# Moving the steps of the weights' sums between the stages of a decoder layer

## The chip, the cores and the metric

The kernel runs on one core of one Trainium2 chip. The metric is the device time of one execution in microseconds (us), the median of the runs shown. All stages run on the same five engines: PE (TensorE, the matmuls), ACT (ScalarE), DVE (VectorE), POOL (GpSimd) and SP (SyncE, which here only issues DMAs). ACT and POOL issue DMAs too, each in the order of its own instructions.

## The reference, cut to what matters

One layer is computed for a prompt of 1024 tokens and for 8 x 8 decode tokens, 1088 columns in all, with a model width of 1024. All is fp32.

```
hn = rmsnorm(x);  u = hn @ w_in                      # q,k,v, gates of both branches
o_a = forgetting attention(q_a, k_a, v_a, logf)      # 8 heads of 64
o_b = gated linear attention(q_b, k_b, v_b, alpha)   # 4 heads, 128 x 256
merged = sigmoid(gate_a) * (o_a @ w_proj_a) + sigmoid(gate_b) * (o_b @ w_proj_b)
x = x + rmsnorm(merged @ w_out)
u = rmsnorm(x) @ w_up;  conv of width 3 over the tokens
y = x + rmsnorm((gelu(g) * a) @ w_down)
```

The product with `w_up` (1024 x 5632) is done for the first 768 tokens with sums of blocks: of each pair of column blocks of `w_up`, four half blocks x11, x12, x21, x22 are added up in four combinations, and these sums take part in seven products instead of eight. The sums depend on the weights alone. They can be made at any time before the stage that multiplies by `w_up`.

## The kernel before, in words

The stages follow each other: the first norm, the forget gates, the attention of the prompt (called FoX here, about 95 to 455 us of the profile), the attention of the decode tokens (to about 640), the linear attention (GLA, four heads, to about 1045), the merge of the branches (to about 1163), the output projection with its norms (to about 1293), the up-projection (to about 1740) and the down-projection. Each fp32 product is made as three products of fp32r halves: `hi` (ACT) and `lo` (DVE or POOL) split an operand, and `three` multiplies.

**The sums of the weights.** They are made by DMAs alone, from HBM to HBM, into the tiles `d_ws[i]`, four of 256 KB for each i from 2 to 21. `ws_step(a, b)` does one step, n = 2, 3, 4 and so on, one n for each call. ACT issues four plain copies of blocks of `w_up` into `d_ws[n]` (L195), placed behind the instruction `a` of ACT. POOL issues up to four adding DMAs (L200), placed behind the instruction `b` of POOL: two from `w_up` into `d_ws[n-1]`, one into `d_ws[n-2]` from a tile of the same i and one into `d_ws[n-3]`, likewise. Each of these waits until the DMA of the step before that wrote its operand has landed. Calls beyond n = 24 issue nothing, and from n = 22 only POOL issues.

**FoX.** Four pairs of heads j; within a pair 16 iterations n, each one tile of 128 queries of a head. In an iteration the scores of the next tile are made (POOL masks the diagonal block, L722, DVE adds and finds the maximum, ACT takes the exponential, L745), then the tile before it is transposed (`pth`, `ptl`) and multiplied with the values. Between these, `slot()` puts in a written-out share of projection matmuls (`mm`), whose weights SP loads (`wraw`) and which hide the softmax; the order of PE's matmuls is fixed by hand. `ws_step(*pace)` is called at n = 1, 4, 7, 10 and 13, with `pace` the last exponential and the last mask. SP also copies `d_sfb`, HBM to HBM, eight times here.

**GLA.** One more call for each head, behind the exponential and the subtraction that make the decayed queries. These are steps 22 to 25.

**The merge.** For each of 8 blocks m of output channels, SP loads the weights (`wraw`, 512 KB), the gate (`sg`, 544 KB) and the first branch's product (`m1`, shown as `m`, 544 KB). ACT takes the sigmoid of `sg` (L1391), PE multiplies in three groups of 384, 384 and 320 columns, and for each group `ev` has DVE multiply by the gate, POOL add `m1`, ACT split off the high half and DVE the low half. `sg` and `m1` have two buffers each, `whi` and `wlo` two, and the PSUM pool of the products three. The operands `bh`, `bl` of the merge are eight blocks k loaded from `d_ob` just ahead of it.

The engines' orders come from a scheduler that walks the program with estimated costs; `tc.issue_after(x)` only says that what is issued in it stands behind x on its engine. DMAs of SP and ACT share eight semaphores in turn, and one that takes a semaphore waits for the DMA that used it before.

Of the kernel before, what the change touches and what calls it, by code (L numbers as in the profile page):

```python
# [10 lines left out]
AF = mybir.ActivationFunctionType  # L11
ALU = mybir.AluOpType
# [7 lines left out]
T = 1024  # L20
# [72 lines left out]
def hybrid_step(ctx, tc, I, O):  # L93
    nc = tc.nc
    pe, act, dve, pool, sp = nc.tensor, nc.scalar, nc.vector, nc.gpsimd, nc.sync
# [10 lines left out]
    def f(ap):  # L106
        return ap.bitcast(F32)
# [19 lines left out]
    def tt(eng, out, a, b, op):  # L127
        eng.tensor_tensor(out=out, in0=a, in1=b, op=op)  # L128
# [7 lines left out]
    def lo(out, src, h, eng=dve):  # L136
        tt(eng, out, src, f(h), ALU.subtract)
# [43 lines left out]
    def ws_step(a, b):  # L181


        n = ws_next[0]
        ws_next[0] += 1

        def x(i):
            wc = [w["w_up"][:, q * P:(q + 1) * P].rearrange("(k p) m -> p k m", p=P) for q in (i, NF + i)]
            return [c[:, k:k + 4] for c in wc for k in (0, 4)]

        with tc.issue_after(a.ins):
            if n in d_ws:
                x11, x12, x21, _ = x(n)
                for d, y in zip(d_ws[n], (x21, x11, x11, x12)):
                    act.dma_start(out=d, in_=y)  # L195
        with tc.issue_after(b.ins):
            for i, d, y in ((n - 3, 3, None), (n - 2, 1, None), (n - 1, 0, 3), (n - 1, 2, 2)):
                if i in d_ws:
                    src = x(i)[y] if y else d_ws[i][{3: 1, 1: 0}[d]]
                    pool.dma_start(out=d_ws[i][d], in_=src, max_dma_last_dim=4 * P * 4, accum_op=ALU.add)  # L200

    ws_next, pace = [2], [None, None]
# [197 lines left out]
    def mgroup(g, wh, wl, evac, M=P, rh=None, rl=None, K=KD):  # L400
        rh, rl = rh or hn_h, rl or hn_l
        o, n = GS[g]
        ps = new(ps_mm, [P, 384], "mm")
        ins = three(ps[:M, :n], [(wh[:, k, :M], wl[:, k, :M], rh[g][:, k, :], rl[g][:, k, :]) for k in range(K)])
        evac(ps, o, n)
        return ins

    def mtile(*args, **kw):
        for g in range(3):
            mgroup(g, *args, **kw)  # L410
# [27 lines left out]
    def w_col(col):  # L438
        return lambda: load_split(wpool, w["w_in"][:, col:col + P], KD, P)
# [27 lines left out]
    def enqueue_fill(n=1):  # L467
        for _ in range(min(n, len(fillers))):
            col, dst = fillers.pop()
            enqueue(w_col(col), lambda dst=dst: spill(dst))  # L470
# [4 lines left out]
    def barrier():  # L475
        bg.append(("B", None))
# [30 lines left out]
    def drain():  # L507
        units(1 << 30)
# [124 lines left out]
    def fox_q(j, t):  # L633

        qd = t["qd"] = [new(foxk, [P, T], f"qd{h}", F32R) for h in range(2)]

        def ev_q(ps, o, n):
            m = min(n, T - o)
            for h in range(2):
                a, b = 64 * h, 64 * (1 - h)  # L640
                act.activation(qd[h][a:a + 64, o:o + m], ps[a:a + 64, :m], AF.Copy, scale=0.125)
                stt(qd[h][b:b + 64, o:o + m], ps[a:a + 64, :m], 0.125, f(qd[h][a:a + 64, o:o + m]),
                    ALU.mult, ALU.subtract)
                if m < n:
                    act.activation(qb[a:a + 64, :, j, 16 * h:16 * h + NS],
                                   ps[a:a + 64, m:n].rearrange("p (b t) -> p b t", t=NS), AF.Copy, scale=0.125)
        return ev_q
# [134 lines left out]
    def fox_jobs(j, t):  # L782
        enqueue(w_col(C_KA + j * P), lambda: fox_kv(j, t, "k"))
        later(lambda: fox_k_out(j, t))
        enqueue(w_col(C_VA + j * P), lambda: fox_kv(j, t, "v"))
        later(lambda: fox_v_out(j, t))
# [10 lines left out]
    for j in range(4):  # L797
        if j < 3:
            fox_jobs(j + 1, tj[j + 1])
        enqueue_fill(FILL_FOX[j])  # L800
        if j < 3:
            barrier()
            enqueue(w_col(C_QA + (j + 1) * P), lambda j=j: fox_q(j + 1, tj[j + 1]))
        slot = spread(SLOTS_FOX + ([8, 4, 4] if j == 3 else []))
        for n in range(16):
            h, qt = 2 * j + n // 8, n % 8
            scores, turn, values = heads[h]
            if n == 7:
                heads[h + 1] = fox_head(j, 1, tj[j])
            if n < 15:  # L810
                heads[2 * j + (n + 1) // 8][0]((qt + 1) % 8)
                if n % 3 == 1:
                    ws_step(*pace)
                slot()
                if qt == 0 and n:
                    heads[h - 1][2](3)
                if qt % 2 == 0 and qt >= 2:
                    values(qt // 2 - 1)
                slot()
                turn(qt)  # L820
                slot()
                if n == 0 and j == 0:
                    suffix_sums()
                if j in (1, 2) and n % 4 == 2:
                    repeat_sums(4 * (j - 1) + n // 4)
            elif j < 3:
                drain()
                bg.pop(0)
                units(4)
                turn(7)  # L830
                fox_split(j + 1, tj[j + 1])
                units(4)
                values(3)
                act.dma_start(out=d_oa[j], in_=tj[j]["oT"])
                units(4)
                heads[h + 1] = fox_head(j + 1, 0, tj[j + 1])
                heads[h + 1][0](0)
            else:
                slot()
                turn(7)  # L840
                slot()
                values(3)
                slot()
                act.dma_start(out=d_oa[j], in_=tj[j]["oT"])
# [203 lines left out]
    with mkpool(name="gla", bufs=1, side="right") as gp:  # L1048
# [9 lines left out]
        for h in range(HB):  # L1058
            q, k, bc = (gh[h][x] for x in ("q", "k", "bc"))
# [123 lines left out]
            drain()  # L1183
            kth, ktl = (new(gp, [P, TT], "wv", F32R, bufs=5)[:, :T].rearrange("p (c t) -> p c t", t=P) for _ in range(2))
            qe = new(gp, [P, TT], "vT")
            pace[0] = act.activation(qe, bc, AF.Exp, scale=1.0 / 16)
            eb = new(gp, [P, 16], "eb")
            dve.tensor_copy(eb[:, :8].unsqueeze(2), qe[:, :T].rearrange("p (c t) -> p c t", t=P)[:, :, P - 1:])
            dve.tensor_copy(eb[:, 8:].unsqueeze(2), qe[:, T:].rearrange("p (c t) -> p c t", t=NS)[:, :, NS - 1:])
# [2 lines left out]
            qh, ql = (new(gp, [P, TT], "wv", F32R, bufs=5)[:, :T] for _ in range(2))  # L1192
# [9 lines left out]
            for i0 in (0, 4, 8):  # L1202
                ps = new(ps_a, [P, 4, P], "tp")
                n, m = (P, 4) if i0 < 8 else (TS, 1)
# [5 lines left out]
                    lo(ktl[:, i0:i0 + m, :], ps, kth[:, i0:i0 + m, :])  # L1210
                else:
                    stack(ps[:n, 0, :], k3, lambda r: (32 * r, None, 64, 32 - 32 * r))
            pace[1] = pool.tensor_tensor(out=ql, in0=qe[:, :T], in1=f(qh), op=ALU.subtract)
            ws_step(*pace)
            sil = []

            def gate(v):
# [152 lines left out]
    with mkpool(name="mg", bufs=2, side="right") as mg, mkpool(name="obp", bufs=1, side="right") as obp:  # L1370
        bh, bl = zip(*([new(obp, [P, KD, n], f"b{x}{g}", F32R) for x in "hl"] for g, (_, n) in enumerate(GS)))
        sg0 = new(mg, [P, TT], "sg")
        for k in range(KD):
            if k in (0, 1):
                raw = new(wpool, [P, UP], "spl")[:, :TT]
            else:
                raw = new(mg, [P, TT], "sg" if k == 4 else "m1")
            sp.dma_start(out=raw, in_=d_ob[k])
            for g, (o, n) in enumerate(GS):
                hi(bh[g][:, k, :], raw[:, o:o + n])  # L1380
                lo(bl[g][:, k, :], raw[:, o:o + n], bh[g][:, k, :], pool if g == 2 else dve)
        drain()
        mh, ml = new_act()
        m2 = last2[0]
        for m in range(KD):
            wh, wl = load_split(wpool, w["w_proj_b"][:, m * P:(m + 1) * P], KD, P)
            sg = new(mg, [P, TT], "sg") if m else sg0
            sp.dma_start(out=sg, in_=d_gb[m])
            m1 = new(mg, [P, TT], "m1")
            sp.dma_start(out=m1, in_=d_m1[m])  # L1390
            act.activation(sg, sg, AF.Sigmoid)  # L1391

            def ev(ps, o, n):
                g = o // 384
                c = slice(o, o + n)
                tt(dve, sg[:, c], ps[:, :n], sg[:, c], ALU.mult)
                tt(pool, sg[:, c], sg[:, c], m1[:, c], ALU.add)
                hi(mh[g][:, m, :], sg[:, c])
                if g < 2:
                    lo(ml[g][:, m, :], sg[:, c], mh[g][:, m, :])  # L1400
                else:

                    lo(ml[g][:, m, :TS], sg[:, T:], mh[g][:, m, 2 * P:])
                    lo(ml[g][:, m, TS:], sg[:, o:T], mh[g][:, m, :2 * P])

            if m == KD - 1:
                load_wo(0, 0, first_wo)
            mtile(wh, wl, ev, rh=bh, rl=bl)
            if m == 2:
                conv_operands()  # L1410

# [374 lines left out]
    with mkpool(name="dr", bufs=1, side="left") as dr, mkpool(name="ds", bufs=1, side="left") as ds, \  # L1786
# [183 lines left out]
        for hf in range(2 * NS_):  # L1970
# [44 lines left out]
            if (name, h) in (("h12", 1), ("s4", 0)):  # L2015
                c = int(name == "s4")
# [38 lines left out]
```

## Time and profile before

| What | Value |
|---|---|
| Runs | 2013.24, 2014.16, 2023.12 us; median 2014.16 |
| Profiled execution | 2014.25 us, its span 2012.5 us |
| Mean granted clock of TensorE | 0.997 |
| Busy: PE, DVE, ACT, POOL | 97%, 65%, 45%, 20% |
| DMA | 335.24 MB, mean 167 GB/s |

The span runs from the first to the last instruction on the core. The busy share of an engine is averaged over all stages. A row of the timeline has its start and its length in us, then engine, line, operation, tiles and shapes, and in brackets the idle time of its engine before it with what ended that.

### The profile page before, as it was taken

The page shows a single profiled execution, that of the slowest core. Times are in us where ns is not written, and L with a number is a line of the kernel's source. Part 1 is how long each engine was busy: PE and PEld are TensorE (multiplying, and loading weights), DVE is VectorE, ACT ScalarE, POOL GpSimd, SP SyncE. Part 2 cuts the span into 40 slices and gives each one's busy share as a digit, 9 for nine tenths or more (in the row PEclk, how much of TensorE's full clock was granted, in tenths as well). Part 3 has the DMA queues.
Part 4 walks back from the last instruction along what each step waited for, and adds up shares of the span by engine and source line. Part 5 has one row for each costly group of instructions (what it writes and reads, how often), then busy time and mean ns, then how long its engine had stood idle before and what let it go on. Part 6 is the DMA issues. An engine that isn't in the chain of part 4 may idle for free.

```text
span 2012.5 us, 35502 instructions
## 1 busy us (share of the span) xinstructions
PE 1952.2 (97%) x13681; PEld 1788.5 (89%) x13681; DVE 1303.1 (65%) x2635; ACT 914.3 (45%) x1762; POOL 411.8 (20%) x582
## 2 busy tenths in 40 slices
PE   6999999999999999999999999999999999999998
PEld 5899989997888988898989977899999999977886
DVE  6566666663333876867564357876777777848685
ACT  5344444453333565564633243454444444545552
POOL 3022323232110111111012211232233233210000
PEclk9999999999999999999999999999999999999999
DMA  4387979797774252323387352134335555667574
GB/s 140 95 195 179 235 177 194 175 230 256 286 267 145 62 130 55 117 60 106 136 273 234 109 172 101 55 120 159 124 127 171 183 170 193 213 191 242 181 250 154
DMA packets 302430, 335.24 MB, mean 167 GB/s; under 512 B 23327, under 2 KB 234575, under 8 KB 298165
## 3 DMA queue, kind: packets, MB, share of 16 engines
q1 hardware_dynamic: 216501, 217.37, 35.0%
q0 software_dynamic: 39488, 79.15, 15.5%
q10 hardware_dynamic: 46272, 36.44, 5.7%
q8 instruction: 108, 1.77, 0.4%
q14 instruction: 61, 0.50, 0.1%
HBM read 265.78 MB, written 113.30 MB: 188 GB/s over the span
## 4 chain that ended last, share of the span: by engine, by line
PE 82%; DVE 6%; DMA 6%; ACT 4%; issue 1%; ACTq 1%; POOL 0%; SPq 0%; DVEq 0%; POOLq 0%
PE mm L122 40%; PE dn L122 15%; PE u L122 9%; PE tp L125 5%; PE o L122 5%; PE S L122 4%; PE y L122 3%; PE sm L122 1%; DMA d_ob<-oo 1%; ACTq L195 1%; DMA smk<-in_consts 1%; DVE wlo L128 1%; DMA m<-d_ob 1%; DVE act L128 0%; ACT whi L134 0%
## 5 line engine op out<-in xcount | busy, mean ns | idle before, releaser
L122 PE MATMUL mm<-act,whi 128*128 128x384 f32 (+2 forms) x3568 | 893.4, 331 | 5.2 <-DVE act L128 3.9
L122 PEld LDWEIGHTS mm<-act,whi 128*128 128x128 f32 (+1 forms) x3568 | 616.8, 188 | 16.6 <-DVE act L128 5.4
L122 PE MATMUL mm<-act,wlo 128*128 128x384 f32 (+2 forms) x1784 | 582.7, 327 | 0.0
L122 PEld LDWEIGHTS mm<-act,wlo 128*128 128x128 f32 (+1 forms) x1784 | 335.8, 188 | 1.7 <-issue 1.2
L128 DVE TENSOR_TENSOR wlo<-wraw,whi 128x1024 fp32r<-128x1024 f32 (+1 forms) x111 | 131.9, 1189 | 57.4 <-ACT whi L134 54.1
L134 ACT ACTIVATE whi<-wraw 128x1024 fp32r<-128x1024 f32 (+1 forms) x113 | 116.0, 1027 | 92.9 <-PE mm L122 85.1
L131 DVE SCALAR_TENSOR_TENSOR cv<-u,cw,cv 128x1104 f32<-128x1104 f32 x84 | 112.7, 1362 | 13.6 <-ACT cv L1555 13.6
L122 PE MATMUL dn<-dh,hhi 128*128 128x512 f32 x264 | 104.9, 399 | 2.4 <-ACT hhi L134 2.4
L122 PE MATMUL dn<-dh,hlo 128*128 128x512 f32 x264 | 104.9, 397 | 0.3 <-DVE hlo L128 0.3
L122 PE MATMUL dn<-dl,hhi 128*128 128x512 f32 x264 | 105.0, 398 | 0.0
L122 PE MATMUL y<-wo,act 128*128 128x512 f32 x416 | 99.8, 397 | 1.6 <-DVE wo L128 1.1
L122 PEld LDWEIGHTS y<-wo,act 128*128 128x128 f32 x416 | 77.1, 188 | 21.5 <-DVE wo L128 2.2
L134 ACT ACTIVATE sh<-sr 128x512 fp32r<-128x512 f32 x80 | 50.6, 633 | 85.7 <-PE u L122 39.9
L722 POOL TENSOR_SCALAR_AFFINE_SELECT bd<-cb 128x128 f32<-128x128 f32 x64 | 36.8, 584 | 182.7 <-DVE mx L739 166.3
L745 ACT ACTIVATE s<-s,ng 128x128 f32<-128x128 f32 (+3 forms) x64 | 49.6, 776 | 49.0 <-DVE ng L743 46.5
L420 ACT ACTIVATE spl<-mm 128x384 f32<-128x384 f32 (+1 forms) x72 | 33.5, 467 | 78.7 <-PE mm L122 77.7
L735 DVE CUSTOM_DVE_ANT_0 s<-S,cb 128x512 f32<-128x512 f32 (+2 forms) x80 | 40.7, 526 | 40.4 <-PE S L122 32.7
L134 ACT ACTIVATE pth<-tp 128x512 fp32r<-128x512 f32 (+2 forms) x96 | 43.5, 488 | 50.8 <-issue 19.7
L122 PE MATMUL mm<-bh,whi 128*128 128x384 f32 (+1 forms) x192 | 63.1, 328 | 2.8 <-ACT bh L134 1.9
L1555 ACT ACTIVATE cv<-u,cw 128x1104 f32<-128x1104 f32 x42 | 54.9, 1310 | 22.0 <-DVE u L131 11.1
L122 PE MATMUL mm<-bl,whi 128*128 128x384 f32 (+1 forms) x192 | 62.9, 327 | 0.1
L122 PE MATMUL mm<-bh,wlo 128*128 128x384 f32 (+1 forms) x192 | 62.6, 327 | 0.3 <-DVE wlo L128 0.3
(470 smaller groups left out, 4210.4 us busy)
## 6 DMA issues: line engine op xcount, KB each, us to landing
wraw<-in_w_in SPq DMA_DIRECT2D x52, 512.0 KB
wraw<-in_w_up SPq DMA_DIRECT2D x44, 512.0 KB
d_ws<-in_w_up ACTq DMA_DIRECT2D x80, 256.0 KB
sr<-d_ws SPq DMA_DIRECT2D x80, 256.0 KB
draw<-in_w_down SPq DMA_DIRECT2D x77, 256.0 KB
d_h<-cv POOLq DMA_DIRECT2D x44, 256.0 KB, 5.0
d_s<-spl POOLq DMA_DIRECT2D x44, 256.0 KB, 5.2
d_ws<-in_w_up POOLq DMA_DIRECT2D x40, 256.0 KB, 8.2
```

Source lines behind the costliest of these rows:

```text
L122: return record(pe.matmul(out, **kw))
L125: return record(pe.transpose(*args))
L128: eng.tensor_tensor(out=out, in0=a, in1=b, op=op)
L131: return dve.scalar_tensor_tensor(out=out, in0=a, scalar=s, in1=b, op0=op0, op1=op1)
L134: act.activation(out, src, AF.Copy)
L195: act.dma_start(out=d, in_=y)
L420: act.activation(t[:, o:o + n], ps[:, :n], AF.Copy)
L722: pace[1] = pool.affine_select(out=bd, in_=cb[:, qc], pattern=[[-1, P]], compare_op=ALU.is_ge, fill=NEG, base=0, channel_multiplier=1)
L735: dve.tensor_tensor_reduce(out=s[:, k0:k0 + m], in0=ps[:, :m], in1=cb[:, k0:k0 + m], scale=1.0, scalar=-3.0e38, op0=ALU.add, op1=ALU.max, ...
L745: pace[0] = act.activation(s[:, :nk], s[:, :nk], AF.Exp, bias=ng, accum_out=sm)
L1555: act.activation(c, u[:, 2:], AF.Identity, scale=cw[:, 2, m:m + 1], bias=cw[:, 3, m:m + 1])
```

## The change

Three of the calls of `ws_step` are placed otherwise; what a step does is the same. In FoX it is called at n = 1, 5, 9 and 13, 16 times instead of 20. In GLA it is no longer called. In the merge it is called after each of the first seven blocks m, with the block's sigmoid on ACT and the block's last addition on POOL as the instructions to stand behind. That makes 23 calls, steps 2 to 24, where there were 24. FoX then issues the copies of i = 2 to 17, the merge those of i = 18 to 21 (m = 0 to 3) and the adding DMAs of steps 18 to 24: four for each of m = 0 to 4, two for m = 5, one for m = 6. The number of DMAs in all stays 80 of each kind.

```diff
--- before.py
+++ after.py
@@ -809,7 +809,7 @@
                 heads[h + 1] = fox_head(j, 1, tj[j])
             if n < 15:
                 heads[2 * j + (n + 1) // 8][0]((qt + 1) % 8)
-                if n % 3 == 1:
+                if n % 4 == 1:
                     ws_step(*pace)
                 slot()
                 if qt == 0 and n:
@@ -1183,7 +1183,7 @@
             drain()
             kth, ktl = (new(gp, [P, TT], "wv", F32R, bufs=5)[:, :T].rearrange("p (c t) -> p c t", t=P) for _ in range(2))
             qe = new(gp, [P, TT], "vT")
-            pace[0] = act.activation(qe, bc, AF.Exp, scale=1.0 / 16)
+            act.activation(qe, bc, AF.Exp, scale=1.0 / 16)
             eb = new(gp, [P, 16], "eb")
             dve.tensor_copy(eb[:, :8].unsqueeze(2), qe[:, :T].rearrange("p (c t) -> p c t", t=P)[:, :, P - 1:])
             dve.tensor_copy(eb[:, 8:].unsqueeze(2), qe[:, T:].rearrange("p (c t) -> p c t", t=NS)[:, :, NS - 1:])
@@ -1210,8 +1210,7 @@
                     lo(ktl[:, i0:i0 + m, :], ps, kth[:, i0:i0 + m, :])
                 else:
                     stack(ps[:n, 0, :], k3, lambda r: (32 * r, None, 64, 32 - 32 * r))
-            pace[1] = pool.tensor_tensor(out=ql, in0=qe[:, :T], in1=f(qh), op=ALU.subtract)
-            ws_step(*pace)
+            lo(ql, qe[:, :T], qh, pool)
             sil = []
 
             def gate(v):
@@ -1388,13 +1387,13 @@
             sp.dma_start(out=sg, in_=d_gb[m])
             m1 = new(mg, [P, TT], "m1")
             sp.dma_start(out=m1, in_=d_m1[m])
-            act.activation(sg, sg, AF.Sigmoid)
+            pace[0] = act.activation(sg, sg, AF.Sigmoid)
 
             def ev(ps, o, n):
                 g = o // 384
                 c = slice(o, o + n)
                 tt(dve, sg[:, c], ps[:, :n], sg[:, c], ALU.mult)
-                tt(pool, sg[:, c], sg[:, c], m1[:, c], ALU.add)
+                pace[1] = pool.tensor_tensor(out=sg[:, c], in0=sg[:, c], in1=m1[:, c], op=ALU.add)
                 hi(mh[g][:, m, :], sg[:, c])
                 if g < 2:
                     lo(ml[g][:, m, :], sg[:, c], mh[g][:, m, :])
@@ -1406,6 +1405,8 @@
             if m == KD - 1:
                 load_wo(0, 0, first_wo)
             mtile(wh, wl, ev, rh=bh, rl=bl)
+            if m < 7:
+                ws_step(*pace)
             if m == 2:
                 conv_operands()
 
```

## Rows read from the trace of the kernel before

**Rows 1.** The page: busy us, share of the span and instructions of each engine.

```profile
PE 1952.2 (97%) x13681; PEld 1788.5 (89%) x13681; DVE 1303.1 (65%) x2635; ACT 914.3 (45%) x1762; POOL 411.8 (20%) x582
```

**Rows 2.** Stretches: busy us by engine, granted clock, DMA share, GB/s.

```profile
95.00:455.00 360.00, 352.97 (x2292) 340.62 (x2292) 225.56 (x686) 159.10 (x353) 101.90 (x143) 1.00 0.86 194
388.00:455.00 67.00, 66.75 (x433) 64.47 (x433) 44.48 (x153) 34.14 (x78) 26.87 (x36) 1.00 1.04 220
640.00:1045.00 405.00, 397.33 (x4163) 357.34 (x4162) 276.30 (x626) 224.64 (x506) 52.54 (x61) 1.00 0.38 110
...
1070.00:1100.00 30.00, 29.18 (x185) 28.62 (x183) 13.06 (x23) 11.47 (x17) 8.79 (x11) 1.00 0.63 181
1100.00:1163.00 63.00, 63.00 (x376) 62.07 (x376) 23.34 (x43) 18.94 (x33) 17.65 (x17) 1.00 0.38 124
```

**Rows 3.** PE's waits, 95 to 455 us: us in total, times, longest.

```profile
PE o L122 <- ACT pth L134: 5.3, 3, 2.7
```

**Rows 4.** ACT's timeline around the first steps of the second and third pair.

```profile
199.55 4.50 ACTq L195 DMA_DIRECT2D d_ws<-in_w_up  x2
204.10 0.38 ACT L134 ACTIVATE pth<-tp 128x256 fp32r<-128x256 f32 x1 [4.96 <-issue]
...
296.45 0.38 ACT L134 ACTIVATE pth<-tp 128x256 fp32r<-128x256 f32 x1 [5.99 <-issue]
```

**Rows 5.** PE's timeline at the same two places.

```profile
204.54 0.39 PE L122 MATMUL o<-pth,vhl 128*128 128x256 f32 x1 [1.72 <-ACT pth L134]
...
296.89 0.39 PE L122 MATMUL o<-pth,vhl 128*128 128x256 f32 x1 [2.71 <-ACT pth L134]
```

**Rows 6.** The tiles d_ws, whole span: duration ns min/median/max, first and last start.

```profile
L195 ACTq DMA_DIRECT2D d_ws<-in_w_up x80: 551/648/4574, 105.3 to 447.6; - x80
...
L200 POOL DMA_DIRECT2D d_ws<-in_w_up x40: 1142/1476/2614, 110.4 to 701.9; - x40
L200 POOL DMA_DIRECT2D d_ws<-d_ws x40: 817/865/1339, 118.7 to 882.9; - x40
...
DMA to landing us min/median/max: 4.3/7.0/14.8
```

**Rows 7.** POOL's timeline after the same step of the second pair.

```profile
207.81 0.82 POOL L200 DMA_DIRECT2D d_ws<-d_ws  x1 [6.70 <-DMA d_ws<-in_w_up]
```

**Rows 8.** The page: DMA queues (SP, POOL, ACT): packets, MB, share of 16 engines.

```profile
q1 hardware_dynamic: 216501, 217.37, 35.0%
q0 software_dynamic: 39488, 79.15, 15.5%
q10 hardware_dynamic: 46272, 36.44, 5.7%
```

**Rows 9.** The merge's timeline, blocks 4 and 5: SP, ACT, DVE, PE.

```profile
1115.17 0.32 SPq L1388 DMA_DIRECT2D sg<-d_gb  x1
...
1123.03 1.11 ACT L1391 ACTIVATE sg<-sg 128x1088 f32<-128x1088 f32 x1 [4.41 <-DMA sg<-d_gb]
...
1124.46 1.04 ACT L134 ACTIVATE whi<-wraw 128x1024 fp32r<-128x1024 f32 x1
...
1125.54 1.22 DVE L128 TENSOR_TENSOR wlo<-wraw,whi 128x1024 fp32r<-128x1024 f32 x1
...
1123.74 0.34 PE L122 MATMUL mm<-bh,whi 128*128 128x384 f32 x1
...
1135.58 0.34 PE L122 MATMUL mm<-bh,whi 128*128 128x384 f32 x1
```

**Rows 10.** The start of the merge: ACT and PE.

```profile
1064.69 1.11 ACT L1391 ACTIVATE sg<-sg 128x1088 f32<-128x1088 f32 x1 [1.46 <-DMA sg<-d_gb]
1067.32 1.30 ACT L134 ACTIVATE bh<-m 128x384 fp32r<-128x384 f32 x3 [1.51 <-DMA m<-d_ob]
...
1067.89 0.45 PE L122 MATMUL mm<-bh,whi 128*128 128x384 f32 x1 [1.92 <-ACT bh L134]
```

**Rows 11.** PE's waits, 640 to 1045 us (GLA).

```profile
PE tp L125 <- DVE oo L128: 2.3, 2, 1.5
```


## The prediction

> **What bounds the kernel now.** I read the page first, for the share of each engine. PE is busy for 1952.2 us, 97% of the span, DVE for 65%, ACT for 45%, POOL for 20% [rows 1]. The next view is the table of busy time by stretch: it shows where PE is idle at all, and so what a moved step can win in each stage [rows 2]. In FoX, 95 to 455 us, PE is busy for 353.0 of 360.0 us, so 7.0 us are idle. In GLA, 640 to 1045, it is 397.3 of 405.0, 7.7 us idle. In the merge from 1070 on, it is 29.2 of 30.0 and then 63.0 of 63.0. Nothing that the change touches stands on a stage with much idle PE.
>
> Third, PE's waits in FoX: the one that counts is for the turned probabilities `pth`, 5.3 us in three waits, the longest 2.7 [rows 3]. The timelines name its cause. At the first step of the second pair of heads ACT issues its third and fourth copy in 4.50 us and then had been idle for 4.96 us, with nothing else that held it; at the same step of the third pair it was 5.99 us [rows 4]. PE stood 1.72 and 2.71 us behind these two holds [rows 5], 4.4 of the 5.3 us. So FoX is bound by PE's own stream, and the steps of the sums cost it something where an issue on ACT takes 3 to 5 us instead of the median of 0.65 us [rows 6].
>
> Last, the queues. The page gives q10 (ACT) 5.7% of 16 engines over the span for 36.44 MB, q0 (POOL) 15.5% for 79.15 MB, q1 (SP) 35.0% for 217.37 MB [rows 8]. Times 2012.5 us and divided by the MB, that is 3.15, 3.94 and 3.24 us of all 16 engines for one MB. One full step, four copies and four additions of 256 KB (1.05 MB each), so takes 3.3 + 4.1 = 7.4 us of all DMA engines.
>
> **The change part by part.** The sum starts from the profiled execution, 2014.25 us: a span of 2012.5 and 1.75 around it. The median of the runs shown is 2014.16, so the two can be used alike.
>
> *FoX, 20 calls to 16.* Four steps leave: 16 issues on ACT (16 x 0.65 = 10 us of an engine that is busy for 159 of 360 us), 16 additions on POOL (8 x 1.48 + 8 x 0.87 = 19 us, busy for 102) [rows 2, 6] and 4 x 7.4 = 30 us of DMA, of 0.86 x 360 = 310 us. Neither ACT nor POOL nor the DMA engines bound the stage, so only PE's idle 7.0 us can be won. The two holds of rows 4 stand at the calls with n = 1, and these stay; so do the calls with n = 13, whose additions POOL issues just ahead of them. What goes is the close pair: the calls at n = 1 and n = 4 follow each other quickly, and POOL waited 6.70 us between them for a DMA of `d_ws` [rows 7]. With n = 5 the distance grows. That wait stood on POOL, not on PE. The bounds: all 7.0 us gone, or one more hold like the longer one (2.7 us more), since the new places n = 5 and 9 can meet another large copy. I take 2.0 us off: a fifth of the 5.3 us, as a fifth of the steps goes, and half of the other 1.7 us of idle PE. If the holds at n = 1 move with the new order of the queues, this term is the one that is off.
>
> *GLA, four calls to none.* Seven additions on POOL go, 2 x 1.48 and 5 x 0.87 = 7.3 us, of an engine that is busy for 52.5 of 405 us [rows 2, 6]. PE's longest group of waits here is for DVE's `oo`, 2.3 us in two [rows 11], and none names POOL. The cover is the idle POOL; with the cover already whole, the removal is worth nothing. Bounds: 2.3 us won, nothing lost, since nothing is added here. I take 0. The subtraction that stays is the same instruction.
>
> *The merge, none to seven.* Sixteen copies on ACT (m = 0 to 3) and 23 additions on POOL (four each for m = 0 to 4, then two and one) come in. I take the copies to be issued right behind each block's sigmoid.
> At m = 0 this meets the one place where PE already waits for ACT: the sigmoid starts at 1064.69 and takes 1.11 us, the last operand block `bh` at 1067.32, and PE stood 1.92 us for it [rows 10]. Four issues of 0.65 us from the sigmoid's end at 1065.80 end at 1068.4, which is 1.1 us past 1067.3. If ACT's queue issues while the sigmoid runs, the cost is 0. If the fourth issue is held for 4.57 us, the longest of rows 6, the end is 1064.69 + 3 x 0.65 + 4.57 = 1071.2, so 3.9 us. I take 1.1.
> For the later blocks, PE's cadence is 1135.58 - 1123.74 = 11.84 us [rows 9]. Behind ACT's issues are queued the high halves of the products and the next weights' `whi`, and behind that DVE's `wlo`, which ends at 1125.54 + 1.22 = 1126.76 while PE needs it at 1135.58: a slack of 8.8 us. One hold of ACT (5.99 at most) fits in it, and so does one of POOL (6.70), whose addition the high half waits for. So blocks 1 to 7 cost 0 as long as the two don't add up with late loads. The DMA engines have room on average: their share is 0.63 from 1070 to 1100 and 0.38 from 1100 to 1163 [rows 2], 42.8 us of 93, to which come four times 7.4 and 7 x 1.03 = 7.2 us, 80 of 93 in all. In FoX the share was 1.04 from 388 to 455 us, and PE was idle for 0.25 of 67 us [rows 2]: a full set of queues alone doesn't hold PE.
>
> *The up-projection.* Its loads of the sums begin far behind the merge, and the DMA of a sum takes 14.8 us at most from issue to landing [rows 6]. The last ones are issued behind block 6, about 1135.58 + 11.84 = 1147.4. That costs 0.
>
> The sum: 2014.25 - 2.0 + 0 + 1.1 = 2013.35. I round it to 2013.4.
>
> **The rivals.**
> *A, FoX gives all back.* All 7.0 us of idle PE in FoX go, the merge costs 0: 2014.25 - 7.0 = 2007.3, and with GLA's 2.3 it is 2005.0. For it: 4.4 us hang on two holds of a queue that gets lighter. Against: those two calls stay where they are, and at the first step of the last pair no such hold is seen though its share of DMA is the highest, so the number of steps isn't what makes them.
> *B, no relief.* The holds at n = 1 are made by the step of n = 13 before them and by other copies at the border of two pairs, all of which stay. FoX gives 0, the merge takes its 1.1: 2015.4. For it: rows 4 and 5. Against: the removed pairs did make POOL wait.
> *C, the loads of the merge come late: slower.* The gate's load takes 1123.03 - 1115.17 = 7.9 us from issue to sigmoid, and ACT already waits 4.41 us for it [rows 9]. A block loads 1.64 MB on SP, 5.3 us of all engines. If three busy queues share alike, that becomes 15.9 us, 4.1 more than the 11.84 us of PE; over m = 0 to 3 that is 16.2 us, of which the slack takes 8.8 and PE 7.4. With the held issue at m = 0: 2014.25 - 2.0 + 3.9 + 7.4 = 2023.6, and with FoX's bad end (+2.7 for -2.0) 2028.3. It decides from the point where a gate lands more than 8.8 us later than now. For it: 5.3 + 7.4 = 12.7 us of DMA for each of the four blocks, over 11.84. Against: two buffers, POOL's additions hold each other back, and rows 2 of 388 to 455.
> The Trainium skill bears on C ("DMA: Bandwidth & Descriptors", section "SWDGE vs HWDGE vs iDMA"): each DMA engine takes its internal queues in turn, and the queues of GpSimd and of SP and ACT are different ones. By that rule the third share, and with it the 2023.6 us, would be what the merge gets while all three are full; no row of this trace shows the shares inside one engine, and its stretch at 1.04 speaks for less.
>
> **How the numbers follow.** The forecast, 2013.4, gets 0.48, B 0.24, A 0.14 and C 0.14. 0.5% of 2014, about 10 us, is what a measurement of this kernel can tell from no change. The forecast and B lie inside it with their bounds (down to 2004.9, up to 2014.25 + 2.7 + 3.9 = 2020.9), and most of A does; below 2004.1 I leave 0.06 (A with an order of the queues that is better in a later stage too). Above 2024.3 lies the worse part of C, 0.10. That leaves 0.84 for no change. The range runs from 2006.0 to 2022.0: it cuts off the far half of A and most of C.
>
> **What would show it.** In FoX, PE's waits for `pth` should fall by a fifth, with the holds at n = 1 of the second and third pair still there; if both are gone, A is right, if neither moved, B. In GLA, POOL loses seven issues and PE nothing. In the merge, the first `bh` wait should grow from 1.92 to about 3 us, the idle time of ACT before the sigmoids should grow, and PE should stay without gaps from block 1 on; gaps of several us there, with `wlo` or the products' evacuation late, are C. The prediction is wrong if PE's idle time from 1045 to 1163 us grows by more than 4 us, or FoX's changes by more than 7.

## Result: slower by 0.5%, and all of it in the merge and the stage of y

| Kernel | Median us | Ratio to before, 95% interval |
|---|---|---|
| before | 2016.70 (14 runs) | 1 |
| changed | 2026.45 (14 runs, 2023.94 to 2029.96) | 1.0053 [1.0041, 1.0065] |

The forecast was 2013.4 us, no change; the measured time lies above its range. The median of 14 runs of before is 2.5 us above the 2014.16 of three runs that the forecast started from; the rest of the miss is the change's. The profiled execution of the changed kernel took 2029.96 us, its span 2028.2.

The stretches of the changed kernel, with the columns of [rows 2]:

```profile
95.00:455.00 360.00, 356.31 (x2319) 344.27 (x2319) 227.84 (x688) 161.84 (x356) 86.13 (x127) 1.00 0.74 173
640.00:1045.00 405.00, 396.26 (x4161) 356.72 (x4160) 278.15 (x629) 225.56 (x508) 46.76 (x56) 1.00 0.36 108
1045.00:1070.00 25.00, 21.63 (x118) 20.96 (x117) 13.62 (x24) 10.27 (x21) 7.59 (x9) 0.93 0.97 321
1070.00:1100.00 30.00, 27.10 (x165) 26.11 (x163) 9.77 (x17) 8.11 (x11) 14.02 (x15) 0.99 1.09 268
1100.00:1114.00 14.00, 7.70 (x30) 7.31 (x31) 2.90 (x6) 4.54 (x12) 6.26 (x9) 0.53 1.08 280
1114.00:1163.00 49.00, 49.00 (x299) 49.00 (x298) 15.97 (x28) 12.23 (x17) 22.28 (x21) 1.00 0.87 191
```

FoX has 3.7 us idle where it had 7.0, GLA 8.7 where it had 7.7. The merge, with 0.8 us idle from 1070 to 1163 before, now has 2.9 us idle from 1070 to 1100 and 6.3 from 1100 to 1114, and in these 14 us the granted clock is 0.53, mostly the lower level of 1.2 GHz. The DMA share rose from 0.63 to 1.09 from 1070 to 1100, and from 0.38 to 1.08 and then 0.87 behind that; the 268 to 280 GB/s up to 1114 are below the 321 that this trace moves from 1045 to 1070.

PE's waits from 1050 to 1180 us of the changed kernel name the place (us in total, times, longest):

```profile
PE mm L125 <- DVE sg L128: 8.4, 3, 5.8
PE y L122 <- ACT wo L134: 2.8, 1, 2.8
PE mm L122 <- ACT bh L134: 2.2, 1, 2.2
```

L125 are the transposes of `conv_operands`, which is called behind block 2 and fills all three PSUM buffers of `mm`. PE's timeline there:

```profile
1097.18 0.52 PE L125 MATMUL mm<-idt,wraw 88*128 88x88 f32 x4 [0.31 <-DVE sg L128]
...
1100.02 0.85 PE L125 MATMUL mm<-idt,wraw 88*128 88x88 f32 x4 [2.32 <-DVE sg L128]
...
1106.62 0.65 PE L125 MATMUL mm<-idt,spl 44*128 44x44 f32 x4 [5.76 <-DVE sg L128]
```

The chain that ended last tells why DVE was late (start us, us, what held the chain):

```profile
1073.61 7.91 PE mm L122 x44
1081.57 12.21 DMA wraw<-in_w_proj_b
1093.86 1.07 ACT whi L134
1094.96 0.39 DVE wlo L128
1095.35 0.75 issue
1096.10 0.57 DVE act L128 x2
1096.72 6.23 DMA sg<-d_gb
1103.06 0.57 ACT sg L1390
1103.67 0.65 ACTq L195
1104.36 0.65 ACTq L195
1105.05 0.53 ACT act L134
1105.60 0.56 DVE act L128
1106.16 0.41 DVE sg L128
1106.62 0.66 PE mm L125 x4
```

Block 3's weights, issued at 1081.57, are in flight for 12.2 us. The same load before was issued at 1080.14 and split at 1088.16, 8.0 us later:

```profile
1080.14 0.40 SPq L273 DMA_DIRECT2D wraw<-in_w_proj_b  x1
...
1088.16 1.06 ACT L134 ACTIVATE whi<-wraw 128x1024 fp32r<-128x1024 f32 x1 [2.83 <-DMA wraw<-in_w_proj_b]
```

Everything that frees a PSUM buffer stands behind them: ACT's queue holds `whi` ahead of the high halves, DVE's holds `wlo` ahead of the low halves and the multiplications by `sg`, and SP issues the next gate only when that low half is done. So one late load becomes a late gate (6.2 us more), then two copies that ACT issues ahead of the high half, and PE at the end of it.

Further on the same chain goes through POOL, up to the wait for `wo` at the start of the stage of y:

```profile
1146.56 6.83 issue
1153.38 0.04 POOLq L200
1153.42 1.79 POOL sg L1396
...
1156.37 6.89 DMA sg<-d_gb
```

POOL stands for 6.83 us with nothing that the view names, up to an instruction of the steps' additions (L200), ahead of an addition of `m1`; the gate that waits for this block's buffer is issued behind it.

From a block's first product to the next one's took 14.8, 12.4, 13.6 and 11.9 us for blocks 0 to 3 before, and 16.1, 12.5, 22.9 and 14.4 now: 13.2 us more, the size of the merge's whole loss. Blocks 2 and 3 hold 11.8 of it. The 1.3 us of block 0 can't be told from spread: a second trace of the kernel before (b2_before, below) has 16.3 us there. Blocks 1 to 7 took 85.2 and 85.3 us in the two traces of before, and 97.2 now.

### The profile page after: what moved, and what is told of

The parts are those of the page before. It is cut to its first block, busy times and chain, and to the rows that moved or that the text cites. A ratio compares the mean times of both kernels' runs of the same rounds, so it can differ in the third digit from the quotient of the medians.

```text
span 2028.2 us, 35492 instructions
## 1 busy us (share of the span) xinstructions
PE 1957.2 (96%) x13681; PEld 1792.2 (88%) x13681; DVE 1303.9 (64%) x2635; ACT 916.4 (45%) x1762; POOL 410.8 (20%) x582
## 4 chain that ended last, share of the span: by engine, by line
PE 78%; DMA 7%; DVE 7%; ACT 4%; issue 2%; POOL 1%; ACTq 1%; SPq 0%; DVEq 0%; POOLq 0%
PE mm L122 38%; PE dn L122 15%; PE u L122 9%; PE tp L125 5%; PE o L122 5%; PE S L122 4%; PE y L122 3%; DMA d_ob<-oo 1%; DMA sg<-d_gb 1%; DMA smk<-in_consts 1%; DMA m<-d_ob 1%; ACTq L195 1%; DVE act L128 1%; DVE wlo L128 1%; DMA wraw<-in_w_proj_b 1%
## 5 line engine op out<-in xcount | busy, mean ns | idle before, releaser
L131 DVE SCALAR_TENSOR_TENSOR cv<-u,cw,cv 128x1104 f32<-128x1104 f32 x84 | 112.9, 1365 | 13.3 <-ACT cv L1556 13.2
L122 PEld LDWEIGHTS dn<-dh,hhi 128*128 128x128 f32 x264 | 49.7, 188 | 14.6 <-ACT hhi L134 3.4
```

The lines of the kernel that those rows point to most:

```text
L122: return record(pe.matmul(out, **kw))
L131: return dve.scalar_tensor_tensor(out=out, in0=a, scalar=s, in1=b, op0=op0, op1=op1)
```

## The experiments

The same marks, read from the timeline of each profiled execution: the start of the first product of the decode rows (FoX's end), and the lengths of GLA, the merge and y, in us, each from its first product to that of the next stage. The up-projection, which follows, takes 471.3 to 471.4 us in each of them. Medians are of 5 to 14 runs, the stages of one execution each. Each ratio compares a kernel with runs of before from the same session, so it isn't the quotient of the medians.

| Kernel | FoX's end | GLA | merge | y | median us | ratio, 95% interval |
|---|---|---|---|---|---|---|
| before | 471.9 | 395.0 | 100.1 | 165.3 | 2016.70 | 1 |
| b2_before | 468.9 | 394.1 | 101.6 | 167.1 | 2016.02 | 1.0004 [0.9982, 1.0025] |
| changed | 467.6 | 396.2 | 113.4 | 169.5 | 2026.45 | 1.0053 [1.0041, 1.0065] |
| e1_gla | 470.5 | 411.8 | 100.4 | 164.7 | 2028.32 | 1.0057 [1.0043, 1.0072] |
| e2_conv_late | 467.1 | 396.6 | 117.4 | 165.9 | 2028.78 | 1.0055 [1.0037, 1.0072] |
| e3_small | 468.1 | 410.7 | 100.7 | 165.8 | 2032.25 | 1.0077 [1.0060, 1.0094] |
| e3_full | 471.0 | 415.7 | 106.6 | 167.6 | 2043.00 | 1.0126 [1.0102, 1.0150] |
| e4_adds | 474.6 | 393.2 | 108.0 | 171.7 | 2029.94 | 1.0069 [1.0054, 1.0084] |
| e5_copies | 467.9 | 394.8 | 101.2 | 166.5 | 2014.54 | 0.9989 [0.9975, 1.0002] |
| e6_up7 | 470.3 | 398.1 | 101.0 | 164.5 | 2010.83 | 0.9972 [0.9958, 0.9986] |
| e8_up15 | 466.3 | 397.7 | 98.8 | 166.4 | 2011.60 | 0.9971 [0.9955, 0.9986] |
| e9_dve_add | 469.4 | 396.5 | 109.6 | 162.1 | 2019.51 | 1.0018 [1.0001, 1.0035] |
| e10_conv_y | 467.8 | 395.0 | 108.4 | 170.1 | 2024.24 | 1.0034 [1.0020, 1.0049] |
| e12_both | 470.9 | 394.9 | 102.4 | 166.5 | 2015.38 | 0.9984 [0.9967, 1.0001] |
| e13_dve_held | 468.9 | 396.2 | 111.0 | 165.1 | 2020.50 | 1.0027 [1.0012, 1.0041] |
| e14_both_held | 469.2 | 395.6 | 105.0 | 163.4 | 2015.60 | 1.0006 [0.9989, 1.0023] |

The spread of one stage between two traces of one kernel is seen in the first two rows: 1.5 us in the merge, 1.8 in y, 3.0 at FoX's end. GLA spreads further: 393.2 to 398.1 us in the traces of kernels without steps in it.

**Is it the merge's steps?** e1_gla puts the seven steps into GLA, one where it was and a second for three of the four heads (cut to the calls, against the changed kernel).

```diff
+            if h < HB - 1:
+                ws_step(*pace)      # GLA, behind the decode rows
-            if m < 7:
-                ws_step(*pace)      # merge
```

> FoX as in the changed kernel (16 steps); the other seven steps in the linear attention: one call for each head as before, and a second one behind the decode rows' copy and the last masked key block of heads 0 to 2; the merge makes none. Theory (the merge's loads come late, PE starves in block 2, its clock falls): FoX keeps its 4.3 us, the merge is back at 100 us from its first product to the output projection's, so 2016.7 - 4 = about 2012.5. Rival (FoX's own order of queues or a later stage costs the time, the merge only shows it): it stays above 2020.

The merge came back to 100.4, as expected, but the sum of about 2012.5 was missed by 16 us: GLA grew by 16.8 us. The loss moved with the steps. In GLA, from 664 to 860 us, DVE and ACT wait for things that the kernel before did not wait for:

```profile
DVE so L131 <- DMA out_gla_s<-so: 9.6, 2, 6.0
```

```profile
ACT spl L420 <- DMA wraw<-in_w_in: 12.9, 2, 7.6
```

Late transfers again: a store of states and a load of weights. That these are what PE lost was not shown; more of that stage was not taken apart.

**Is it the place of `conv_operands`?** e2_conv_late calls it behind block 5 instead of block 2.

```diff
-            if m == 2:
+            if m == 5:
                 conv_operands()
```

> The changed kernel with one edit: the operands of the convolution are made after block 5 of the merge instead of block 2, when the copies on ACT are over. Theory (block 2's stall comes from the three PSUM buffers that these transposes take while DVE is behind a late weight load): PE's gap of 10 us in block 2 goes and with it most of the half clock, the merge falls from 113 to about 103 us, the time to about 2017. Rival (the DMA load alone starves PE): the gap stays in blocks 2 and 3, 2024 or more.

Missed: the merge is 117.4. PE still waits 10.0 us at the transposes, now behind block 5, where additions are still running, and 3.9 us at products before them.

**Is it the issues or the bytes?** e3_small and e3_full are e1_gla with DMAs on scratch tiles in the merge, of 8 or of all 128 rows (cut).

```diff
+        act.dma_start(out=d[c], in_=y[c])
+        pool.dma_start(out=d_xs[i][d][c], in_=src[c], ..., accum_op=ALU.add)
```

> The first kernel of this call, and in the merge the same DMAs in number, order and waits as the changed kernel has there, but on scratch tiles and of 8 of 128 rows (16 KB instead of 256 KB), so issue and waiting without the bytes. Theory (the bytes make the loads late): the merge takes at most 2 us longer than in the first kernel. Rival (the issues on ACT and POOL, and the shared semaphores, hold the in-order queues): PE's gap in block 2 is there and the time is 8 us or more above the first kernel.

> The kernel of e3_small (16 steps in FoX, seven in the linear attention, and in the merge the same number, order and waits of DMAs as in the changed kernel, on scratch tiles), but each of these DMAs now moves its whole 256 KB instead of 8 of 128 rows. Theory (the merge's own loads come late because of the bytes that the copies and additions move): the merge, 100.7 us with small DMAs, becomes about as long as in the changed kernel, 113 us (110 to 117), with waits of ACT for wraw of about 6 us and PE waits before the first transposes of conv_operands; the whole is then 2032 + 13 = 2045 us. Rival (the loss of the changed kernel comes from the order of queues that FoX and GLA leave behind, not from the bytes in the merge): the merge stays at 101 to 104 us and the whole at about 2032.

Both texts say "the same number"; that holds for the 16 copies, but the additions of these two are 16, where the changed kernel has 23. With 8 rows the merge stays at 100.7: issues and their places on ACT and POOL cost nothing. An addition held POOL for a median of 1.43 and 0.78 us there (from `w_up` and from a tile), 1.80 and 0.83 with all rows, so its issue was kept nearly whole. With all rows the merge is 106.6. So bytes are needed for a loss, and 106.6 instead of the expected 113 may go with 4.2 MB of additions for 6.0.

**Copies or additions?** e4_adds leaves the copies in FoX (20 calls at every third tile) and has the additions alone in the merge; e5_copies leaves the merge's additions out, so that the last sums are incomplete there.

```diff
-            for i, d, y in ((n - 3, 3, None), (n - 2, 1, None), ...
+            for i, d, y in () if n > 17 else ((n - 3, 3, None), ...
```

> The changed kernel with the copies of all 20 blocks issued in FoX at the old places (n = 1, 4, 7, 10, 13), the additions as in the changed kernel (16 steps in FoX, seven in the merge). Theory: additions are a little over half of the bytes' engine time, so about half of the merge's loss stays, merge 104 to 108 us, and FoX loses part of its gain: 2018 to 2022. Rival (the copies on ACT alone do it, since ACT waits at the gate): merge 100 to 102 us.

> The changed kernel with the merge's additions left out (the sums of the last steps stay incomplete); its copies, 16 of 256 KB in blocks 0 to 3, stay. The merge was 113.4 us with both, 100.1 before, and 108.0 with the additions alone (e4_adds). Theory (the bytes in blocks 0 to 3 delay the loads, whoever moves them): 16 copies of the 39 DMAs take 3.3 of each step's 7.4 us, so the merge becomes about 105 us (103 to 108), the whole about 2018 (2016 to 2021). Rival 1 (POOL, held while it issues additions, is what delays): the merge is back at 100 to 102 and the whole 2012. Rival 2 (copies on ACT are the whole loss): merge 111 to 114.

Copies alone: 101.2, not told from before; the theory of bytes "whoever moves them" missed with its 105, and rival 1, POOL, had the number. Additions alone: 108.0, as expected for the merge; but the whole, 2029.94 for an expected 2018 to 2022, was missed. FoX ends 5.5 us behind the mean of the kernels with 16 steps there, with 8.2 us of PE's waits for `pth`, and y takes 171.7. What sets copies and additions apart in the profile is the price. The DMA queues of the changed kernel from 1057 to 1170 us (packets, MB, share of 16 engines):

```profile
q1 hardware_dynamic: 11680, 15.99, 45.0%
q0 software_dynamic: 7122, 6.00, 36.1%
q10 hardware_dynamic: 8448, 4.20, 12.8%
```

Share times 113 us over MB: q1 (SP) 3.18, q10 (ACT) 3.44, q0 (POOL) 6.80 us of all engines per MB. An added MB takes twice the engine time of a copied one. The shares of all queues in these 113 us add up to 0.54 before, 0.64 in e5_copies, 0.86 in e4_adds and 0.94 in the changed kernel, in the order of the merge's length: 100.1, 101.2, 108.0, 113.4. That goes with engine time as the cause, but doesn't prove it: whether copies of as much DMA time would cost as much was not tried.

**Bytes, or POOL that is held while it issues additions?** e9_dve_add does the merge's addition of `m1` on DVE, so that no evacuation stands in POOL's queue; e10_conv_y moves `conv_operands` to the stage of y; e12_both does both.

```diff
-                pace[1] = pool.tensor_tensor(out=sg[:, c], in0=sg[:, c], in1=m1[:, c], op=ALU.add)
+                pace[1] = dve.tensor_tensor(out=sg[:, c], in0=sg[:, c], in1=m1[:, c], op=ALU.add)
...
             ins = y_half(i, half)
+            if t == 6:
+                conv_operands()
```

> The changed kernel, but the merge's addition of m1 to the gated product is done by DVE instead of POOL, so that no evacuation stands behind POOL's queue, on which the seven steps' 23 additions are issued; the steps and their bytes stay. e5_copies showed that the copies alone cost the merge nothing (101.2 us), so the loss of 13 us hangs on the additions. Theory (their traffic keeps the weights' and gate's loads in flight for up to 12 us, which lets DVE's in-order queue and the PSUM buffers run late): the merge stays long, 108 to 115 us, with ACT's wait of about 6 us for wraw and PE's wait before conv_operands, whole 2020 to 2028. Rival (POOL, held 3 to 7 us while it issues additions, delays the evacuations): the merge comes back to 100 to 103, whole about 2012 to 2015.

> The changed kernel, but conv_operands (its two loads, twelve transposes in three PSUM buffers of mm, and their evacuations) is called in the stage of y, behind its seventh product, and not after block 2 of the merge; the y stage then holds those 1.6 us of PE. Theory (a block may run up to about 9 us late before PE sees it; the transposes, which need all three buffers at once, take that reserve in one step): the merge falls to 100 to 106 us, with the late wraw load of about 12 us still there, y at 166 to 169, whole about 2014 to 2018. Rival (the late loads starve PE wherever the transposes stand, as in e2_conv_late with 117): merge 110 to 117, whole 2024 or more.

> Both edits at once: the merge's addition on DVE, and conv_operands in the stage of y; the steps are where the changed kernel has them. If late loads and the taken PSUM reserve explain the loss, no more is gained over e10_conv_y than 0 to 2 us. If POOL's hold is a cause of its own, this one falls to 100 to 101 us in the merge and about 2012 in all, below e10_conv_y by 3 us or more.

Each alone takes 4 to 5 us off the merge; with `conv_operands` 1.7 us of PE's own work leave it for y (block 2 took 13.6 us before, blocks 4 to 7 took 11.8). e9_dve_add lies where its theory had it; e10_conv_y missed its 100 to 106 and, with 2024.24, its 2014 to 2018: without the transposes PE waits at the products themselves, 6.5 us in six. Both together come to 102.4, which speaks for POOL, but e9 and e12 changed a second thing: with nothing on POOL to hold them, seven of the 23 additions started at 437 to 462 us, so these two had only 16 in the merge. So e13_dve_held and e14_both_held hold all 23 in the merge, by a copy of one column on POOL:

```diff
+                tt(dve, sg[:, c], sg[:, c], m1[:, c], ALU.add)
                 hi(mh[g][:, m, :], sg[:, c])
+                if g == 2:
+                    pace[1] = pool.tensor_copy(mark, f(mh[g][:, m, :1]))
```

> As e9_dve_add (the merge's addition of m1 on DVE), but a copy of one column on POOL, behind each block's last high half, holds the steps where the changed kernel has them: in e9_dve_add seven of the 23 additions had started at 437 to 459 us, long before the merge, since nothing on POOL held them, so that kernel changed two things. Theory (bytes: 23 additions in the merge at 6.8 us of all engines per MB keep the loads late, POOL's hold is secondary): merge 110 to 114, as in the changed kernel. Rival (POOL's hold of the evacuations is a cause of its own): merge 104 to 109, no longer than e9_dve_add's 109.6.

> e13_dve_held and conv_operands in the stage of y, with all 23 additions in the merge. e10_conv_y had 108.4 us in the merge with POOL's addition, e12_both 102.4 with DVE's and 16 additions. Theory (bytes): 107 to 110 in the merge, as e10_conv_y, whole 2021 to 2025. Rival (POOL's hold): 101 to 104, whole about 2015.

e13 at 111.0 lies where the theory of bytes had it: POOL's hold alone isn't what makes the merge long. Its blocks 1 to 7 take 97.5 us, as in the changed kernel. e14 at 105.0 lies between the two: 6 us less than e13 by the place of `conv_operands`, of which 1.7 only went to y, and 3.4 less than e10 by POOL's hold, 2.7 without block 0. What the addition on DVE gives back lies more in y: 4.4 us from the changed kernel to e13, 6.7 from e10 to e14. In its time e14, with every DMA of the changed kernel still in the merge, is no slower than before. But its stage of y is also shorter than that of before, 163.4 us with the transposes in it, and the kernel before with the same two edits was not run; so this doesn't show that the steps cost nothing there. The stretches of e14 show how full its queues are:

```profile
1070.00:1100.00 30.00, 29.15 (x176) 28.57 (x175) 12.44 (x23) 8.58 (x11) 9.32 (x11) 1.00 1.11 294
1100.00:1163.00 63.00, 58.80 (x341) 58.33 (x341) 29.82 (x58) 17.49 (x26) 17.16 (x20) 0.95 0.94 206
```

DMA at 1.11 and 0.94, and PE idle for 5.1 us of 93, where the changed kernel had 9.2. What is left of the loss stands in one block, the seventh, which takes 18.9 us instead of 11.8. There it is again a late load: the first weights of the next stage, whose halves stand ahead of the evacuations on ACT and DVE:

```profile
1130.07 9.55 DMA wraw<-in_w_out
1139.64 1.06 ACT wo L134
1140.73 1.22 DVE wo L128
```

So the loss goes with one source, loads that are late beside the additions, and with one way to PE, evacuations that stand behind those loads in the queues of ACT and DVE. Calling `conv_operands` behind block 2 brings it forward, and POOL's hold adds to it, in y more than in the merge. Moving `conv_operands` moves three things at once, which no run separates: transposes that need all PSUM buffers, three small loads on SP just ahead of block 3's weights, and one of the two `wraw` buffers, which its operand takes.

**How much of FoX's gain is real?** b2_before is the kernel before once more.

> The kernel before once more, for a second trace of it: how much each stage varies between two traces of one kernel. FoX's end (first product of the decode stage) stood at 471.9 us in the first; the six traces of kernels with 16 steps in FoX stand at 467.1 to 471.0. If the gain of FoX is real, this one is at 471 to 473; if it is spread between executions, at 467 to 470. The merge is expected at 100 us again, GLA at 395.

468.9, the side of "spread". Twelve traces with 16 steps in FoX (all but those of e4 and e8) stand at 467.1 to 471.0, mean 469.1; the two of before at a mean of 470.4. A gain of about 1 us can't be told from nothing by this mark. PE's wait for `pth` says a little more: 5.3 us in [rows 3] and 3.9 in b2_before with 20 steps, 2.4 to 4.3 with a mean of 3.1 in the twelve with 16, and 1.1 in e8_up15 (below) with eight. It falls with the steps, by some 1.5 us from 20 to 16, though single traces overlap.

**A place where the steps are free.** e6_up7 has 16 steps in FoX and seven in the up-projection, e8_up15 eight and 15.

```diff
             ca = conv(last[0], last[1])
+            if i < 9:               # e8_up15: i < 17
+                ws_step(*pace)      # behind conv's activation and POOL copy
```

> 16 steps in FoX as in the changed kernel, none in GLA and the merge, the last seven in the up-projection, one in each of its first seven rounds, behind the activation and the copy of conv. Theory (seven steps cost something only where the stage's own loads are on PE's path; the up-projection moves 0.4 to 0.5 of the DMA engines' time and PE never waits there): FoX keeps its gain of about 4 us, the merge is back at 100 us, GLA at 395 to 396, the up-projection unchanged at 471: 2016.7 - 4 = about 2012 (2009 to 2016). Rival (wherever 16 copies and 23 additions go in, they cost PE 10 us or more): the up-projection grows by 10 us or more, about 2025.

> Eight steps in FoX (every eighth tile), the other 15 in the up-projection, one in each of its first 15 rounds. Theory: FoX had 7.0 us of idle PE before and lost some 4 of them with a fifth of the steps gone; with 12 more gone it gains 5 to 7 us over before, the up-projection stays at 471 although its DMA share rises from 0.45 to about 0.75: 2016.7 - 6 = 2011 (2008 to 2014). Rival (the holds in FoX don't depend on the number of steps): no more than e6_up7, 2012 to 2016. Rival 2 (the up-projection's loads of weights and sums come late at such a share): it grows by 5 us or more, above 2018.

Both beat both kernels: 0.28% and 0.29% under before, with intervals below 1, and some 0.7 to 0.8% under the changed kernel. Where the gain of e6_up7 lies, its stages don't show: the execution that was profiled took 2017.68 us, far above its median, and no stage in it is clearly shorter than before. The up-projection of e8_up15:

```profile
1330.00:1500.00 170.00, 170.00 (x1038) 170.00 (x1037) 123.57 (x161) 75.97 (x114) 75.40 (x127) 1.00 0.95 238
1500.00:1700.00 200.00, 200.00 (x1225) 200.00 (x1224) 148.10 (x189) 83.68 (x127) 86.58 (x143) 1.00 0.77 217
```

PE is busy for all 370 us at DMA shares of 0.95 and 0.77. Additions cost nothing here. What differs is the distance of the loads: in e8_up15 SP issues weights at 1397.48 whose split ACT starts at 1416.74, 19.3 us later and not held by them, in rounds of 21.6 us. ACT does wait for late sums, 53.0 us in ten waits over the stage, but PE waits for nothing. In the merge ACT comes to the split of block 3's weights 5.7 us behind their issue at 1081.57, and then waits:

```profile
1093.86 1.06 ACT L134 ACTIVATE whi<-wraw 128x1024 fp32r<-128x1024 f32 x1 [6.62 <-DMA wraw<-in_w_proj_b]
```

That this distance is what decides is argued from these rows; no run changed it alone. FoX has 357.39 of 360 us busy in e8, against 356.31 in the changed kernel, and 352.97 [rows 2] and 354.60 in the two traces of before.

## Why the prediction was wrong

**The step that failed is the merge's term of 1.1 us, and in it first the balance of the DMA engines, by its price of an addition.** The merge grew by 13.3 us, 11.8 against the second trace of before. "3.15, 3.94 and 3.24 us of all 16 engines for one MB" took q0 from the page [rows 8]. That row mixes the additions (80 of 0.262 MB, 21 MB) with 58 MB of plain stores of POOL. Additions by themselves stand in FoX of the kernel before, 95 to 455 us, where the queues read:

```profile
q0 software_dynamic: 25104, 19.14, 38.5%
```

0.385 x 360 / 19.14 = 7.24 us per MB; 6.80 in the merge. A step is then 3.3 + 7.6 = 10.9 us instead of 7.4, and the balance 42.8 + 4 x 10.9 + 7 x 1.9 = 99.7 us of 93, not "80 of 93 in all". The merge had no "room on average". That alone doesn't give the loss: e14, with the same DMAs, has 5.1 us of PE idle in the merge instead of 9.2.

**The slack of 8.8 us was counted for one late thing at a time, and for the wrong user.** "Blocks 1 to 7 cost 0 as long as the two don't add up with late loads": they add up. The slack is that of the weights up to the product that uses them, and block 3's late `wlo` ended at 1096.2, about when PE would have needed it without the waits. What came late were the evacuations of the block before, since `whi` and `wlo` stand ahead of them in the queues of ACT and DVE; and the reserve of three PSUM buffers is spent at once by `conv_operands`, which the prediction didn't look at. From e13 to e14 its move gives back 5.9 us of the merge, 4.2 beyond its own work on PE.

**Rival C was what happened, at 0.14, with its number partly by luck.** It priced 2023.6 to 2028.3; measured 2026.45. Late loads and late evacuations came as it said. But its sum took 7.4 us from blocks that each run 4.1 us late, 3.9 at m = 0 and, at its upper end, a loss in FoX; the runs showed nothing clear at m = 0, no loss in FoX and 11.8 us in blocks 2 and 3. The objection to it, "rows 2 of 388 to 455", was no evidence: SP's queue took only 13.4% of the engines there, and weights that SP issued at 390.19 were split at 424.45, 34 us later, so full queues cost nothing there, as in the up-projection of e8_up15. The queues of the changed kernel from 1080 to 1094 us, when block 3's weights were in flight:

```profile
q0 software_dynamic: 1276, 0.91, 44.5%
q1 hardware_dynamic: 2105, 1.57, 39.6%
q10 hardware_dynamic: 2873, 1.43, 35.2%
```

and those of e5_copies in the same stretch:

```profile
q1 hardware_dynamic: 3111, 2.53, 60.6%
q10 hardware_dynamic: 2613, 1.29, 31.3%
```

With additions present SP's queue moved 1.57 MB in 14 us instead of 2.53 (2.50 before). The Trainium skill ("DMA: Bandwidth & Descriptors", section "SWDGE vs HWDGE vs iDMA") says that an engine takes its internal queues in turn. The shares of time agree with it roughly, 44.5, 39.6 and 35.2%; the packets, 1276, 2105 and 2873, aren't equal, and that all three queues were full all the time isn't shown. e10 to e14 show that a load's lateness isn't yet the loss.

**The other terms.** GLA at 0: right (396.2 against 395.0 and 394.1). m = 0 at 1.1: the wait for `bh` was 2.2 us, between the 1.92 and 2.58 of the two traces of before, so nothing is seen of the term; ACT issued the first copy at 1060.45, while the sigmoid of 1060.42 still ran, which is the prediction's case of 0. The up-projection at 0: right, 471.4. FoX at -2.0: the wait for `pth` went from 5.3 and 3.9 in the two traces of before to 2.4, and FoX's end moved by 1.3 us on the mean of all traces; not told from zero, so B's term fits as well. The two holds at n = 1 are still there, as forecast, but PE stood only 0.50 and 1.43 us behind them, where it was 1.72 and 2.71 [rows 5], and 1.62 and 1.07 in b2_before. Not foreseen at all: y, which took 2 to 4 us more; PE waited 2.8 us for `wo` behind the chain through POOL shown above, and the granted clock behind that wait was 0.83 from 1170 to 1180. The mark that the prediction set itself, idle time from 1045 to 1163 us growing by more than 4 us, was met: 3.2 to 12.6 us.

## What to carry to other kernels

Price a DMA by a window in which its kind is alone on its queue, not by the queue's row of the whole page. Before moving background transfers into a stage, count how far ahead of their use that stage's own loads are issued, in time, and what else stands in the in-order queues behind them; the busy share of PE or of the DMA engines doesn't tell it: at a share of 0.95 PE lost nothing where weights were issued 19.3 us ahead of their split, and the merge lost 12 to 13 us where ACT came to a split 5.7 us behind the issue.

## What the runs showed of the hardware

An accumulating DMA, DRAM to DRAM, took 6.8 to 7.2 us of all engines per MB (the changed kernel's merge, before's FoX), a copy 3.4. With all three queues at work the sum of their shares went to 1.19 at 279 GB/s (1080 to 1094 us of the changed kernel), where SP's queue alone moved 310 GB/s at 0.96 (before, 1045 to 1070). Shares that add up to more than 1 count some time twice, so these prices are what the profile books, not an engine's own time.

The clock took its share of the loss. Among the waits of 8.4 us at the transposes PE was busy for 1.4 of the 4 us from 1096 to 1100, and from 1100 to 1110 the granted clock was 0.50. From 1100 to 1114 it was 0.53, so PE ran its products at 1.2 GHz just when it had become late (mean ns of one, after the busy us):

```profile
L122 PE MATMUL mm<-bh,whi 128*128 128x384 f32 x8 | 3.9, 492 | 0.5 <-DVE cw L1353 0.5
L122 PE MATMUL mm<-bl,whi 128*128 128x384 f32 x7 | 3.3, 475 | 0.0
L122 PE MATMUL mm<-bh,wlo 128*128 128x384 f32 x7 | 3.3, 469 | 0.0
```

Before, in the same window, these three took 331, 328 and 328 ns, so 22 products cost about 22 x 0.15 = 3.3 us more. With the waits of 8.4 us that is 11.7 of the 11.8 us that blocks 2 and 3 grew by. e13_dve_held, with 7.4 us of waits there, had 0.59 in that window; e5_copies, with none, had 1.00 from 1070 to 1163.
